# Loading the first third of an image-rotation kernel as four runs of consecutive rows, and storing it as four transfers

## The chip, the cores and the metric

The kernel runs on one core of one Trainium2 chip. The metric is the device time of one execution in microseconds (us). Before the change three executions took 122.31, 122.42 and 122.51 us, so the median is 122.42 us.

## The reference

The input is 32 images of 3 channels, each plane 256 x 256 in fp32: 96 planes of 65,536 values, 25.17 MB. The reference turns every plane by 180 degrees:

```python
def reference(x):
    return np.rot90(x, k=2, axes=(-2, -1)).astype(np.float32)
```

A turn by 180 degrees of a plane in row-major order is nothing but the plane's 65,536 values in reverse order. Every byte is read once from HBM and written once, so 50.33 MB must move.

## The kernel before

The 96 planes are cut into three groups of 32 (`G = 32`). A plane is cut into four quarters of `E = 16384` values, 64 KiB each, and a quarter is called a row here. A group is then 128 rows, one for each partition of SBUF: row 4n + s is quarter s of plane n. Three tiles A, B (`Bt`) and C (`Ct`) of 128 partitions x 16384 values hold the three groups, and a small tile T of 128 x 2048 is scratch. All four lie in SBUF at the same time, so no group waits for a buffer.

Two steps make the turn. Inside a row, VectorE reverses the 16384 values in place. `swap(t, lo, w)` does it for one pair of column blocks, in three copies (line 52): the upper block backwards into T, the lower block backwards into the upper one's place, and T into the lower one's place. `inside(t)` does four such swaps, each of `J = 2048` columns. Between rows, the store reverses the order of the four quarters of a plane: its HBM side is `o4[g][:, ::-1, lo:hi]`, three nested indices, 32 planes by 4 quarters (backwards) by the columns.

The first group is loaded by four transfers (line 73), each with every fourth row, into every fourth partition; two are issued by SyncE's queue (SP in the profile) and two by ScalarE's (ACT). Partition p receives row p. The loads of B and C (line 55) are one transfer of 128 rows each, on SP's queue.

VectorE's copies are kept in program order. It does three whole swaps of A and part of the fourth, then all of B, then the last 1152 columns on each side of A (`LAST = 1152`), then all of C. The stores (line 58) are all issued by SP, in program order: a strip of A of 128 columns, 512 B of each row (`LEAD = 128`), which needs only the first swap of A; then the other 16256 columns of A, which need the last copy of A and so stand behind all of B's swaps; then B; then C. A store waits on SP for the copies and loads that it needs, and everything behind it on SP waits with it.

Of the kernel before, what the change touches and what calls it, by code (L numbers as in the profile page):

```python
# [2 lines left out]

os.environ.setdefault("NEURON_RT_ULTRASERVER_MODE", "4")

# [4 lines left out]


@with_exitstack
def kernel(
    ctx: ExitStack,
    tc: tile.TileContext,
    x: bass.AP,
    out: bass.AP,
):

    nc = tc.nc
    P = 128

    B, C, H, W = x.shape
    L = H * W
    G = 32
    E = L // 4
    J = E // 8

    x4 = x.rearrange("b c h w -> (b c) (h w)").rearrange(
        "(g n) (s e) -> g (n s) e", n=G, s=4)
    o4 = out.rearrange("b c h w -> (b c) (h w)").rearrange(
        "(g n) (s e) -> g n s e", n=G, s=4)  # L40

    pool = ctx.enter_context(tc.tile_pool(name="slots", bufs=1))
    A = pool.tile([P, E], x.dtype, tag="A")
    Bt = pool.tile([P, E], x.dtype, tag="B")
    Ct = pool.tile([P, E], x.dtype, tag="C")
    T = pool.tile([P, J], x.dtype, tag="T")

    def back(t, lo, hi):
        return t[:, hi - 1:(lo - 1 if lo else None):-1]

    def copy(dst, src):
        tc.keep_in_program_order(nc.vector.tensor_copy(out=dst, in_=src))  # L52

    def load(t, g, lo, hi, queue=nc.sync):
        return queue.dma_start(out=t[:, lo:hi], in_=x4[g][:, lo:hi])

    def store(t, g, lo, hi):
        return nc.sync.dma_start(
            out=o4[g][:, ::-1, lo:hi], in_=t[:, lo:hi])

    def swap(t, lo, w):
        hi = E - lo - w
        copy(T[:, 0:w], back(t, hi, hi + w))
        copy(t[:, hi:hi + w], back(t, lo, lo + w))
        copy(t[:, lo:lo + w], T[:, 0:w])

    def inside(t):
        for lo in range(0, E // 2, J):
            swap(t, lo, J)

    SPLIT = 4
    for i in range(SPLIT):
        (nc.sync, nc.scalar)[i % 2].dma_start(  # L73
            out=A[i::SPLIT, :], in_=x4[0][i::SPLIT, :])
    load(Bt, 1, 0, E)
    load(Ct, 2, 0, E)
    LAST = 1152
    LEAD = 128
    for lo in range(0, E // 2 - J, J):
        swap(A, lo, J)  # L80
    swap(A, E // 2 - J, J - LAST)
    store(A, 0, 0, LEAD)
    inside(Bt)
    swap(A, E // 2 - LAST, LAST)
    store(A, 0, LEAD, E)
    store(Bt, 1, 0, E)
    inside(Ct)
    store(Ct, 2, 0, E)


# [1 line left out]
_INS = ['x']  # L92
_OUTS = [((32, 3, 256, 256), 'float32')]


# [23 lines left out]
```

## Time and profile before

| what | value |
|---|---|
| median of three executions | 122.42 us |
| the profiled execution's own time | 122.3 us |
| span of its trace | 120.5 us |
| VectorE busy | 44.6 us (37%) |
| bytes moved | 50.33 MB |
| mean rate over the span | 418 GB/s |

Only two kinds of work show in the page: VectorE's 39 copies and the transfers. The span is the time between the first and the last record of the program; 1.8 us of the profiled execution's time lie around it. The page's row of DMA digits gives the mean busy share of the core's 16 DMA engines in 40 slices. The row of rates below it is in lumps, because a 64 KiB packet counts where it starts, so a rate is to be read over many microseconds. A packet is one contiguous piece that a DMA engine moves; the smallest ones, under 512 B, are the marks by which the engines report that their share of a transfer is done.

### The profile page before, as it was taken

The page shows a single profiled execution, that of the slowest core. Times are in us where ns is not written, and L with a number is a line of the kernel's source. Part 1 is how long each engine was busy: PE and PEld are TensorE (multiplying, and loading weights), DVE is VectorE, ACT ScalarE, POOL GpSimd, SP SyncE. Part 2 cuts the span into 40 slices and gives each one's busy share as a digit, 9 for nine tenths or more (in the row PEclk, how much of TensorE's full clock was granted, in tenths as well). Part 3 has the DMA queues.
Part 4 walks back from the last instruction along what each step waited for, and adds up shares of the span by engine and source line. Part 5 has one row for each costly group of instructions (what it writes and reads, how often), then busy time and mean ns, then how long its engine had stood idle before and what let it go on. Part 6 is the DMA issues. An engine that isn't in the chain of part 4 may idle for free.

```text
span 120.5 us, 101 instructions
## 1 busy us (share of the span) xinstructions
DVE 44.6 (37%) x39; POOL 0.2 (0%) x4
## 2 busy tenths in 40 slices
DVE  0000000299991099999849999500000000000000
POOL 0000000000000000000000000000000000000000
DMA  9888998899889988998889777988898889888980
GB/s 348 348 348 348 522 522 348 348 479 566 348 348 479 566 348 348 479 566 348 348 367 691 345 345 345 691 348 348 348 696 348 348 348 696 348 348 348 674 370 0
DMA packets 1056, 50.33 MB, mean 418 GB/s; under 512 B 160, under 2 KB 288, under 8 KB 288
## 3 DMA queue, kind: packets, MB, share of 16 engines
q1 hardware_dynamic: 960, 46.14, 88.5%
q10 hardware_dynamic: 96, 4.19, 8.6%
HBM read 25.17 MB, written 25.17 MB: 418 GB/s over the span
## 4 chain that ended last, share of the span: by engine, by line
DMA 33%; DVE 27%; another core or an unknown queue 1%; SPq 1%; issue 1%; DVEq 0%
DMA Bt<-in_x_dram 33%; DVE T L52 9%; DVE Bt L52 8%; DVE Ct L52 8%; DVE A L52 1%; SPq L73 1%; DVEq L52 0%
## 5 line engine op out<-in xcount | busy, mean ns | idle before, releaser
L52 DVE COPY T<-A 128x2048 f32<-128x2048 f32 (+2 forms) x5 | 5.1, 1014 | 23.4 <-DMA A<-in_x_dram 23.3
L52 DVE COPY T<-Bt 128x2048 f32<-128x2048 f32 x4 | 4.9, 1227 | 5.9 <-DMA Bt<-in_x_dram 5.8
L52 DVE COPY T<-Ct 128x2048 f32<-128x2048 f32 x4 | 4.9, 1227 | 2.0 <-DMA Ct<-in_x_dram 1.9
L52 DVE COPY A<-T 128x2048 f32<-128x2048 f32 (+2 forms) x5 | 5.1, 1013 | 0.2
L52 DVE COPY A<-A 128x2048 f32<-128x2048 f32 (+2 forms) x5 | 5.1, 1013 | 0.2
L52 DVE COPY Bt<-Bt 128x2048 f32<-128x2048 f32 x4 | 4.9, 1227 | 0.1
L52 DVE COPY Bt<-T 128x2048 f32<-128x2048 f32 x4 | 4.9, 1227 | 0.1
L52 DVE COPY Ct<-T 128x2048 f32<-128x2048 f32 x4 | 4.9, 1227 | 0.1
L52 DVE COPY Ct<-Ct 128x2048 f32<-128x2048 f32 x4 | 4.9, 1226 | 0.1
L103 POOL MEMSET const-bfloat16-1.0<- 128x1 bf16 x1 | 0.1, 101 | 0.0
L103 POOL MEMSET const-uint8-127<- 128x1 uint8 x1 | 0.1, 101 | 0.0
L103 POOL MEMSET const-float32-0.0<- 128x1 f32 x1 | 0.1, 98 | 0.2 <-issue 0.2
L103 POOL MEMSET const-float32-1.0<- 128x1 f32 x1 | 0.1, 98 | 0.0
## 6 DMA issues: line engine op xcount, KB each, us to landing
out_dram<-A SPq DMA_DIRECT2D x1, 8128.0 KB, 21.1
out_dram<-A SPq DMA_DIRECT2D x1, 64.0 KB, 34.8
A<-in_x_dram ACTq DMA_DIRECT2D x2, 17.1
A<-in_x_dram SPq DMA_DIRECT2D x2, 17.3
Bt<-in_x_dram SPq DMA_DIRECT2D x1, 40.1
Ct<-in_x_dram SPq DMA_DIRECT2D x1, 58.8
out_dram<-Bt SPq DMA_DIRECT2D x1, 39.8
out_dram<-Ct SPq DMA_DIRECT2D x1, 42.7
```

Source lines behind the costliest of these rows:

```text
L52: tc.keep_in_program_order(nc.vector.tensor_copy(out=dst, in_=src))
L73: (nc.sync, nc.scalar)[i % 2].dma_start(out=A[i::SPLIT, :], in_=x4[0][i::SPLIT, :])
L103: nc = _bacc.Bacc("TRN2", target_bir_lowering=False, num_devices=1)
```

## The change

The four loads of A still fill every fourth partition each, but load i now reads 32 consecutive rows of the input, rows 32i to 32i + 31, that is planes 8i to 8i + 7. So partition 4k + i now holds row 32i + k, where before partition p held row p.

Because the planes now lie elsewhere in A, one transfer can no longer store A as before. Four transfers store it, all issued by SP after A's last swap: transfer i takes the 32 partitions i, i + 4, i + 8, ... and writes planes 8i to 8i + 7, again with the four quarters of each plane backwards. Its HBM side is 8 planes by 4 quarters by 16384 values. The 512 B strip is gone, and whole rows are stored. VectorE's copies, the loads and stores of B and C and the queues are as before.

```diff
     SPLIT = 4
     for i in range(SPLIT):
         (nc.sync, nc.scalar)[i % 2].dma_start(
-            out=A[i::SPLIT, :], in_=x4[0][i::SPLIT, :])
+            out=A[i::SPLIT, :], in_=x4[0][i * G:(i + 1) * G, :])
     load(Bt, 1, 0, E)
     load(Ct, 2, 0, E)
     LAST = 1152
-    LEAD = 128
     for lo in range(0, E // 2 - J, J):
         swap(A, lo, J)
     swap(A, E // 2 - J, J - LAST)
-    store(A, 0, 0, LEAD)
     inside(Bt)
     swap(A, E // 2 - LAST, LAST)
-    store(A, 0, LEAD, E)
+    N = G // SPLIT
+    for i in range(SPLIT):
+        nc.sync.dma_start(
+            out=o4[0][i * N:(i + 1) * N, ::-1, :], in_=A[i::SPLIT, :])
     store(Bt, 1, 0, E)
     inside(Ct)
     store(Ct, 2, 0, E)
```

## The prediction

> **What bounds the kernel now.** I read the page first: shares of the engines, the 40 slices, the packet counts, and the list of DMA issues.
>
> ```profile
> span 120.5 us, 101 instructions
> DVE 44.6 (37%) x39; POOL 0.2 (0%) x4
> ...
> DMA  9888998899889988998889777988898889888980
> ...
> DMA packets 1056, 50.33 MB, mean 418 GB/s; under 512 B 160, under 2 KB 288, under 8 KB 288
> ```
>
> VectorE works 37% of the span; the DMA digits stay at 7 to 9 from the first slice to the last but one. So the transfers bound the kernel throughout. The last line will matter most. This kernel issues ten transfers (four loads of A, one each of B and C, two stores of A, one each of B and C), and 160 packets are under 512 B: 16 for each transfer, one for each DMA engine. The 128 packets of exactly 512 B are the strip, the difference between 160 and 288. What remains, 768, are the rows: 6 passes of 128.
>
> The stretches of the trace give the pace (the last two columns are the mean busy share of the 16 engines and the rate):
>
> ```profile
> 4.00:19.00 15.00, 0.00 (x0) 0.00 (x0) 1.00 0.97 419
> ...
> 24.00:36.00 12.00, 11.62 (x12) 0.00 (x0) 1.00 1.01 437
> ...
> 60.50:61.20 0.70, 0.00 (x0) 0.00 (x0) 1.00 1.56 625
> ...
> 82.00:116.00 34.00, 0.00 (x0) 0.00 (x0) 1.00 1.00 432
> ```
>
> Loads (4 to 36 us) and stores (82 to 116 us) run at one pace, 432 GB/s at a share of 1.00: 27.0 GB/s for an engine, and 65,536 B by that is 2.43 us for one row on one engine. Around 61 us, where loads end and stores begin, no engine shows a hole (the share above 1 is the lumps of packets counted where they start).
>
> The issues and the order on SP's queue say when each third lands:
>
> ```profile
> out_dram<-A SPq DMA_DIRECT2D x1, 8128.0 KB, 21.1
> out_dram<-A SPq DMA_DIRECT2D x1, 64.0 KB, 34.8
> A<-in_x_dram ACTq DMA_DIRECT2D x2, 17.1
> ...
> Ct<-in_x_dram SPq DMA_DIRECT2D x1, 58.8
> out_dram<-Bt SPq DMA_DIRECT2D x1, 39.8
> out_dram<-Ct SPq DMA_DIRECT2D x1, 42.7
> ```
>
> ```profile
> 2.89 0.47 SPq L55 DMA_DIRECT2D Ct<-in_x_dram  x1
> ...
> 59.13 0.76 DVE L52 COPY A<-T 128x1152 f32<-128x1152 f32 x1
> 59.92 0.57 SPq L58 DMA_DIRECT2D out_dram<-A  x1
> 60.53 0.60 SPq L58 DMA_DIRECT2D out_dram<-Bt  x1
> ...
> 76.92 0.54 SPq L58 DMA_DIRECT2D out_dram<-Ct  x1
> ```
>
> C's load lands at 2.89 + 58.8 = 61.7, A's store at 59.92 + 21.1 = 81.0, B's at 60.53 + 39.8 = 100.3, C's at 76.92 + 42.7 = 119.6. Each stored third takes 19.3 us: 128 rows over 16 engines are 8 rows each, 8 x 2.42 = 19.3. The transfers of one queue go through in the order of issue, and each is issued well before its turn. Nothing but the engines' pace and how evenly rows are dealt over them sets the end.
>
> **The change part by part.** I sum against the profiled execution: span 120.5 us, 1.8 us around it, 122.3 us, which is 0.1 us under the median.
>
> *Loads of A from consecutive rows.* Same packets, same partitions, same queues; only the HBM addresses differ. The nearest rows are the loads of B and C, which read consecutive rows: 437 GB/s against 419 for A. The 8.39 MB of A take 20.0 us at 419 and 19.2 at 437, so a gain of up to 0.8 us; no row shows a loss, and I allow the same 0.8. I take 0, since at 419 the engines are already 0.97 busy.
>
> *The strip.* Its 64 KiB move with the whole rows instead, and 128 packets, 16 marks and one issue of SP go. At the pace above 64 KiB are 0.15 us. Against that, the strip lay ready in the queue behind C's load and covered the joint. A's store is issued at 59.92. The kernel's first load is issued at 0.73 and nothing moves before 2 us, about 1.3 us later, so stores may start about 61.2, and the loads land up to 61.7. Bounds -0.2 to +0.5 us; I take 0.
>
> *Issues on SP.* In the changed program's order on SP, where one store of A stood after the last swap there are now four. The first waits for VectorE's last copy of A, at the same 59.9 us, since no VectorE instruction is moved; the other three wait besides only for loads long landed. At 0.6 us each (0.57 and 0.60 above) they end at 62.3, so B's store is issued about 1.8 us later. B's rows are behind A's on any engine that has A's rows: one of the new transfers is at least 2 rows, 4.8 us, and covers three issues of 1.8 us. C's store waits for VectorE until 76.9, as before. Cost 0, unless some engines get no row of A; those would idle about 2 us, but they would also be far ahead.
>
> *How the new stores are dealt.* This is the term that counts. The outermost index of the transfers before is 32 or 128 on both sides: 32 x 4 planes and quarters against 128 partitions in the stores, 32 against 32 or 128 against 128 rows in the loads. All are multiples of 16, and all left 16 marks. In the changed program a store of A is 8 x 4 x 16384 on its HBM side and 32 rows on its SBUF side. No row of this trace shows an outermost 8. Lower bound: the 32 rows are dealt over 16 engines, as in the four loads of A, 2 each, and the cost is 0. Upper bound with rows at their present pace: planes are dealt whole, 8 engines take 4 rows each and the other 8 none. Four such transfers give the eight 16 rows instead of 8: 8 more x 2.42 = +19.3 us. The rest of the kernel does not return this, because B's and C's rows are dealt evenly and the eight busy engines still have 8 rows of each to do: from 61.3 they have 16 + 8 + 8 = 32 rows, 77.4 us, to about 138.7, against 24 before. The other eight finish near 63.6 + 16 x 2.42 = 102 and stand idle. I take the upper value: the nearest row in form is the store of B, whose outermost index on the HBM side is the plane, and there 32 planes are two whole planes for each engine; nothing in the trace shows a plane cut between engines.
>
> [...]
>
> *Sum.* 122.3 + 0 + 0 + 0 + 19.3 = 141.6 us.
>
> **The rivals.**
>
> *Rows are still dealt over 16 engines.* For it: the loads of A, the same 32 rows and partitions, did so. Against it: their outermost index is 32 on both sides. The point that decides is the number of marks of a new store, 16 or 8. Then only the small terms remain: 122.3 us, between 121.3 and 123.6. This is the case that is not slower.
>
> *Eight engines, and they get in each other's way in SBUF.* With planes dealt whole, engine c reads partitions 16c + i, then 4, 8 and 12 further, all eight in step and at few places at a time. If two share a path that carries one engine's 27.0 GB/s, a row of A takes 4.84 us while they collide: 16 x 2.42 = +38.7 us more at most for pairs, 180.3 us. Against it: the loads of A also touch every fourth partition and lose nothing (419 GB/s at 0.97). For it: those were spread over 16 engines by a deal that the trace does not show. Anything between 142 and 180 is possible, as far as engines fall out of step.
>
> [...]
>
> *Eight engines, but 432 GB/s is a limit of all together.* Then the eight would go faster once the others are idle, from about 102 us. They have 15 rows left each; in half the time that gives back 18 us: 123.5 us. Against it: an engine is busy 1.00 of the time at its 27.0, with no waiting that another's idleness could remove.
>
> **How the numbers follow.** Chances: the forecast 0.52, collisions 0.33, 16 engines 0.10, the shared limit 0.05. The forecast alone has 140.8 to 143 us: its small terms are -0.8 - 0.2 and +0.8 + 0.5. The range must take in most of the collisions: 140 to 181 us leaves out the 0.15 of the two fast cases and some 0.05 of collisions by more than pairs. A difference under 0.2% is what a measurement here can't tell from none. Slower takes the forecast, collisions and the shared limit, 0.90; the case of 16 engines is split into faster 0.04, same 0.04 and slower 0.02: together faster 0.04, same 0.04, slower 0.92.
>
> **What would show it.** In the profile after, packets under 512 B: twelve transfers would leave 192 with 16 engines each, 160 if the four stores of A leave 8 each. The DMA digits stay at 9 until about 102 us and then fall to 5, at about 216 GB/s, until the end. The stores of A land about 99 us, B's at 119, C's at 138.7. If instead A's stores land at 138 the collisions are there; if they land at 81 the deal is over 16. VectorE's copies must stand where they stood. The prediction is wrong if the marks are 192, or if the rows' pace after 61 us is not 27.0 GB/s for each busy engine.

## The result

The changed kernel takes 179.44 us (median of four executions, 179.35 to 179.66) against 122.45 us in the same comparison. The ratio is 1.4659, with a 95% interval of 1.4634 to 1.4685. The time lies inside the range of 140 to 181 us, near its upper end, but the loss is 57.0 us where 19.3 were forecast.

The page of the changed kernel:

```profile
span 177.9 us, 102 instructions
DVE 44.6 (25%) x39; POOL 0.2 (0%) x4
...
DMA  7999799999799909998999889954544543222120
...
DMA packets 928, 50.33 MB, mean 283 GB/s; under 512 B 160, under 2 KB 160, under 8 KB 160
```

VectorE's work is the same 44.6 us. The marks are 160, not 192: eight transfers with 16 marks and four with 8, so each new store runs on eight engines. The DMA digits fall to 5 after some 115 us and then to 2 from some 150 us: first eight engines, then four still have rows to do.

The stretches of its trace (the last two columns are the mean busy share of the 16 engines and the rate in GB/s):

```profile
4.00:19.00 15.00, 0.00 (x0) 0.00 (x0) 1.00 0.97 419
...
61.50:66.50 5.00, 4.13 (x4) 0.00 (x0) 1.00 0.51 105
...
72.00:100.00 28.00, 5.23 (x5) 0.00 (x0) 1.00 0.98 309
...
120.00:140.00 20.00, 0.00 (x0) 0.00 (x0) 1.00 0.50 213
150.00:172.00 22.00, 0.00 (x0) 0.00 (x0) 1.00 0.25 110
```

Two of these lines have the same share and not the same rate. From 61.5 to 66.5 us, when A's stores have begun and B's have not, eight engines are busy and move 105 GB/s, 13 GB/s each. From 120 to 140 us eight engines are busy and move 213 GB/s, 27 each. So busy engines do not move at one pace: right after 61.5 us each row takes twice as long. From 72 to 100 us all sixteen are busy, eight with A and eight with B and C, at 309 GB/s where such a stretch had 432 before.

The issues:

```profile
Ct<-in_x_dram SPq DMA_DIRECT2D x1, 59.1
out_dram<-Bt SPq DMA_DIRECT2D x1, 90.5
out_dram<-Ct SPq DMA_DIRECT2D x1, 99.5
```

```profile
60.44 6.58 SPq L85 DMA_DIRECT2D out_dram<-A  x4
...
67.06 2.63 SPq L58 DMA_DIRECT2D out_dram<-Bt  x1
...
77.40 0.57 SPq L58 DMA_DIRECT2D out_dram<-Ct  x1
```

B's store lands at 67.06 + 90.5 = 157.6 us and C's at 77.40 + 99.5 = 176.9: 19.3 us apart, as before. Going back another 19.3 us, the last engine was done with A at about 138.3, where 100.0 would be the end at the full pace (61.3 + 16 x 2.42). The loads end where they did, within 0.6 us. So all of the loss lies in A's stores: they last 77 us on the slowest engine, a mean of 4.8 us for a row.

The mean hides the course. The trace also keeps the time of every packet, and each row's packet begins where another one ends, so the rows of one engine can be followed. On the engine that ends last the first two rows take 5.1 and 5.3 us, the next six 7.0 to 8.4 us, and all 24 after them 2.42 us each. Altogether 21 rows take over 6 us. They lie on the four engines that end last, and all of them begin between 71 and 112 us, while the rows of B and C run on the other eight engines (from 70.4 to some 120 us).

### The profile page after: what moved, and what is told of

Same layout as the page of the kernel before. It is cut to its first block, busy times and chain, and to the rows that moved or that the text cites. A ratio compares the mean times of both kernels' runs of the same rounds, so it can differ in the third digit from the quotient of the medians.

```text
span 177.9 us, 102 instructions
## 1 busy us (share of the span) xinstructions
DVE 44.6 (25%) x39; POOL 0.2 (0%) x4
## 5 line engine op out<-in xcount | busy, mean ns | idle before, releaser
L52 DVE COPY T<-A 128x2048 f32<-128x2048 f32 (+2 forms) x5 | 5.1, 1013 | 23.9 <-DMA A<-in_x_dram 23.8
## 6 DMA issues: line engine op xcount, KB each, us to landing
out_dram<-Bt SPq DMA_DIRECT2D x1, 90.5
out_dram<-Ct SPq DMA_DIRECT2D x1, 99.5
```

## The experiments

One theory and three rivals stood at this point. Theory: the eight engines of one new store, and those that store B beside them, read SBUF at partitions that share a path. Rivals: the HBM side (eight engines writing planes 256 KiB apart), the loads' new order, or four small transfers as such.

**The loads alone.**

```diff
-            out=A[i::SPLIT, :], in_=x4[0][i::SPLIT, :])
+            out=A[i::SPLIT, :], in_=x4[0][i * G:(i + 1) * G, :])
```

with the strip and the store of A as before.

> The loads of A read consecutive rows as in the changed kernel; A is stored as before, strip and then one transfer with 32 planes outermost (so A's planes go out in another order than the reference wants). If the new addresses of the loads matter by no more than the 0.5 us by which VectorE's first copy starts later after the change (23.8 against 23.3 us), this takes 122.4 to 123.0 us. If the loads' order is what costs, it takes 130 us or more.

Measured 122.53 us, ratio 1.0013 (1.0003 to 1.0022). The loads' order costs 0.16 us by the ratio.

**Four stores, 32 rows outermost.** To the changed kernel:

```diff
+    r4 = out.rearrange("b c h w -> (b c) (h w)").rearrange(
+        "(g n) (s e) -> g (n s) e", n=G, s=4)
...
-            out=o4[0][i * N:(i + 1) * N, ::-1, :], in_=A[i::SPLIT, :])
+            out=r4[0][i * G:(i + 1) * G, :], in_=A[i::SPLIT, :])
```

> The changed kernel with the same four stores of A, the same partitions and the same 2 MB of HBM each, but the HBM side written as 32 rows in place of 8 planes by 4 quarters (the quarters of A are not turned round, which is left out). If the outermost 8 narrows a store to eight engines and everything follows from that, this takes 122.3 to 123.2 us, with 192 packets under 512 B. If the cost lies in having four transfers of 32 partitions, in every fourth partition, or in SP's issues, it stays between 140 and 180 us.

Measured 122.73 us, ratio 1.0027 (1.0011 to 1.0043), with these packets:

```profile
DMA packets 960, 50.33 MB, mean 416 GB/s; under 512 B 192, under 2 KB 192, under 8 KB 192
```

The same four pieces of 2 MB, from the same partitions, cost next to nothing once the outermost size is 32: 192 marks, sixteen engines each. The whole loss hangs on the outermost 8.

**Eight engines, neighbouring partitions.** To the changed kernel:

```diff
-            out=A[i::SPLIT, :], in_=x4[0][i * G:(i + 1) * G, :])
+            out=A[i::SPLIT, :], in_=x4[0][i::SPLIT, :])
...
-            out=o4[0][i * N:(i + 1) * N, ::-1, :], in_=A[i::SPLIT, :])
+            out=o4[0][i * N:(i + 1) * N, ::-1, :], in_=A[i * G:(i + 1) * G, :])
```

> The loads of before (partition p holds row p); four stores of 8 planes each, as in the changed kernel on the HBM side, but from 32 neighbouring partitions, so that each engine reads four neighbouring partitions and no two of the eight read 32 apart. Theory, paired places in SBUF: the eight no longer slow each other, the narrow deal remains, and only the last two stores of A (partitions 64 to 127) can meet the stores of B on the other eight engines; 141.6 us if they do not meet, about 161 us if they share by halves while they meet. The rate just after 62 us is 216 GB/s at a share of 0.5. Rival, the HBM side (eight engines writing planes 256 KiB apart): HBM is addressed exactly as after the change, so the rate after 62 us is 105 GB/s at 0.5 and the time stays near 179 us.

Measured 163.19 us, ratio 1.3339 (1.3317 to 1.3361). HBM is written exactly as in the changed kernel, on eight engines too, and 16 us of the loss are gone. The time is near the 161 us that were expected if A's last two stores and B's rows share by halves while they meet. The rival of the HBM side falls. The stretches of this run show what is left:

```profile
62.00:78.00 16.00, 14.44 (x12) 0.00 (x0) 1.00 0.84 360
82.00:118.00 36.00, 0.00 (x0) 0.00 (x0) 1.00 0.99 204
```

Until 78 us A's first two stores (partitions 0 to 63) run beside B's store at a rate that fits the share (0.84 of 432 is 363). From 82 to 118 us, with A's other two stores (partitions 64 to 127), all sixteen engines are busy at less than half the rate: there each row takes 4.7 to 5.4 us.

**Five ways to store A, with nothing beside them.** Each way starts when the one before it has landed, through a one-column copy into A (`after_all()`; the calls between the ways are left out here):

```python
    for i in range(4):        # 1
        nc.sync.dma_start(out=o4[0][i * 8:(i + 1) * 8, ::-1, :], in_=A[i::4, :])
    for i in range(4):        # 2
        nc.sync.dma_start(out=o4[1][i * 8:(i + 1) * 8, ::-1, :], in_=A[i * G:(i + 1) * G, :])
    for i in range(4):        # 3
        nc.sync.dma_start(out=r4[2][i * G:(i + 1) * G, :], in_=A[i::4, :])
    for i in range(2):        # 4
        nc.sync.dma_start(out=o4[0][i * 16:(i + 1) * 16, ::-1, :], in_=A[i::2, :])
    store(A, 1, 0, E)         # 5
```

> Five ways to store the 8.39 MB of A, one after another with nothing beside them, each separated by a wait for the one before (nothing is reversed, the content is not the reference's). 1: as in the changed kernel, 8 planes from every fourth partition. 2: 8 planes from 32 neighbouring partitions. 3: 32 rows from every fourth partition. 4: two transfers of 16 planes from every second partition. 5: one transfer as before the change. Theory, paired places: 77 us for 1 if the pairs stay in step (eight engines at half pace) and less if they fall out of step, 38.7 us for 2, 19.3 us for 3 and 5, and up to 38.7 us for 4, where sixteen engines read, two at a time 32 partitions apart. Rival, HBM side: 1 and 2 alike, 4 and 5 alike. Rival, narrow deal alone: 38.7, 38.7, 19.3, 19.3, 19.3 us, and the loss of the changed kernel would come only from B's stores beside A's.

The timeline of this run, where each copy ends one way, and the brackets hold VectorE's wait for it:

```profile
73.93 0.15 DVE L52 COPY A<-T 128x1 f32<-128x1 f32 x1 [51.08 <-DMA out_dram<-A]
...
115.00 0.15 DVE L52 COPY A<-T 128x1 f32<-128x1 f32 x1 [40.92 <-DMA out_dram<-A]
...
136.50 0.15 DVE L52 COPY A<-T 128x1 f32<-128x1 f32 x1 [21.35 <-DMA out_dram<-A]
...
177.37 0.15 DVE L52 COPY A<-T 128x1 f32<-128x1 f32 x1 [40.72 <-DMA out_dram<-A]
177.56 0.57 SPq L58 DMA_DIRECT2D out_dram<-A  x1
```

Way 3 waits 21.35 us: 19.3 for the rows, some 2 for issue and landing. Way 5, the single store of before, is issued at 177.56, and the span ends at 199.5, 21.9 us later: the full pace too. Way 2, eight engines from neighbouring partitions, takes 19.6 us more: the narrow deal, at the forecast's price. Way 1, the changed kernel's, takes another 10.2 us. Way 4 is the telling one: sixteen planes outermost, and still 40.72, with rows of up to 5.4 us. If each engine takes a whole plane, the sixteen read in pairs 32 partitions apart, and the doubled time would come from these pairs even though no engine is without rows. That is the author's reading, since the trace names no partition. But way 1 should have taken 77 us if its pairs had stayed in step; it waits 51.08.

**Two engines alone.** Three stores of 2 planes in each of five phases, from 8 partitions that lie 1, 2, 4, 8 and 16 apart (`after_all()` as above):

```python
    for step in (1, 2, 4, 8, 16):
        after_all()
        for k in range(3):
            nc.sync.dma_start(
                out=o4[n // 32][n % 32:n % 32 + 2, ::-1, :],
                in_=A[0:7 * step + 1:step, :])
            n += 2
```

> Two engines alone: A is loaded, and then five phases, each waiting for the one before, of three stores of 2 planes from 8 partitions, which lie 1, 2, 4, 8 and 16 apart (nothing is reversed and most of the output is not written). Each engine reads 12 rows of a phase, the two always 4, 8, 16, 32 and 64 partitions apart, on the same HBM addresses' pattern in all phases. If places are paired 32 apart and nowhere else, four phases take 12 x 2.42 = 29 us and some 2.3 us of issue and landing, and the fourth (32 apart) up to 58 us, less if the two fall out of step. If any two engines that read few partitions slow each other, all five are slow.

```profile
53.67 0.15 DVE L52 COPY A<-T 128x1 f32<-128x1 f32 x1 [30.88 <-DMA out_dram<-A]
84.97 0.15 DVE L52 COPY A<-T 128x1 f32<-128x1 f32 x1 [31.14 <-DMA out_dram<-A]
116.44 0.15 DVE L52 COPY A<-T 128x1 f32<-128x1 f32 x1 [31.32 <-DMA out_dram<-A]
157.02 0.15 DVE L52 COPY A<-T 128x1 f32<-128x1 f32 x1 [40.43 <-DMA out_dram<-A]
```

The distances are those of the author's reading, a whole plane of four rows for each engine: 4, 8, 16, 32 and 64 partitions. Two engines 4, 8 and 16 apart take 31 us, and 32 apart 40.4. The stretches below show the first phase, three parts of the fourth, and the fifth, in which 64 apart again moves 56 GB/s. Of these distances only 32 costs time, with 26 GB/s for the pair at first. Inside the fourth phase the two drift out of step:

```profile
24.00:52.00 28.00, 0.00 (x0) 0.00 (x0) 1.00 0.13 56
118.00:128.00 10.00, 0.00 (x0) 0.00 (x0) 1.00 0.10 26
128.00:140.00 12.00, 0.00 (x0) 0.00 (x0) 1.00 0.11 38
140.00:154.00 14.00, 0.00 (x0) 0.00 (x0) 1.00 0.11 47
158.00:186.00 28.00, 0.00 (x0) 0.00 (x0) 1.00 0.13 56
```

The pair together moves 26 GB/s at first, one engine's worth, then 38, then 47. The packets show the same: the first row of each takes over 5 us, the last ones 2.42, and one engine ends at 154.1 us, the other at 156.6, one row later. By then one engine has got ahead by a row.

**A's stores by themselves in the kernel.** To the changed kernel:

```diff
-    store(Bt, 1, 0, E)
     inside(Ct)
+    copy(A[:, 0:1], T[:, 0:1])
+    copy(T[:, 0:1], Bt[:, 0:1])
+    copy(Bt[:, 0:1], T[:, 0:1])
+    copy(T[:, 0:1], Ct[:, 0:1])
+    copy(Ct[:, 0:1], T[:, 0:1])
+    store(Bt, 1, 0, E)
     store(Ct, 2, 0, E)
```

> The changed kernel with the stores of B and C held back until all four stores of A have landed (five one-column copies on VectorE between them, which rewrite one column of A, so that the store of it is waited for, and of B and C with their own values). Theory: in the phases run the same four stores of A took 51.2 us by themselves, from their first issue to the next phase's, so most of what A's stores lose in the changed kernel comes from B's stores on the other eight engines, which read the same places. Then, from the issue at 60.4 us: 51.2 + 0.5 + 41.2 (two stores over sixteen engines, 38.7, and 2.5 for issue and landing) is a span of 153.3 and a time of 155 us: holding transfers back makes the kernel 24 us faster. Rival, the eight engines' pairs alone cost it all: A's stores still land near 138 us and the time is about 182 us.

Measured 155.53 us, ratio 1.2703 (1.2683 to 1.2722), span 153.4. The kernel with less overlap is 23.9 us faster than the changed one. A's last store has landed when VectorE's first held copy starts:

```profile
60.23 6.58 SPq L85 DMA_DIRECT2D out_dram<-A  x4
...
111.28 0.15 DVE L52 COPY A<-T 128x1 f32<-128x1 f32 x1 [34.12 <-DMA out_dram<-A]
...
111.84 0.61 SPq L58 DMA_DIRECT2D out_dram<-Bt  x1
```

That is 51.1 us after the first issue, against 77.9 us (60.44 to about 138.3) when B's and C's rows are read beside them. No row takes over 5.3 us here, where 8.4 was the longest in the changed kernel.

**The same with neighbouring partitions.** The five copies in the kernel that takes 163.2 us.

> The same holding back, with the four stores of A from 32 neighbouring partitions (163.2 us without it). Theory: the narrow deal alone is left; 59.9 + 41.1 (phase 2 of the phases run) + 0.5 + 41.2 is a span of 142.7 and a time of 144.5 us. Rival, the rows of 5.1 us after 80.8 us in that run come from the partitions 64 to 127 themselves and not from meeting B's: about 166 us.

Measured 145.23 us, ratio 1.1866 (1.1849 to 1.1882), span 143.1. With B held back, the engines keep 206 GB/s at a share of 0.48 from 62 to 98 us, 26.8 for each busy engine. The slow stretch after 82 us was B's and A's rows meeting, not the partitions 64 to 127 themselves.

**The strip.**

```diff
-    LEAD = 128
...
-    store(A, 0, 0, LEAD)
...
-    store(A, 0, LEAD, E)
+    store(A, 0, 0, E)
```

> The kernel before without the strip: A stored whole in one transfer after its last swap. The forecast's term for the strip was 0, between -0.2 and +0.5 us: 122.2 to 122.9 us.

Measured 122.50 us, ratio 1.0010 (1.0001 to 1.0019): 0.1 us.

**Four stores by quarters.** To the changed kernel:

```diff
-            out=A[i::SPLIT, :], in_=x4[0][i * G:(i + 1) * G, :])
+            out=A[i::SPLIT, :], in_=x4[0][i::SPLIT, :])
...
-    N = G // SPLIT
...
-            out=o4[0][i * N:(i + 1) * N, ::-1, :], in_=A[i::SPLIT, :])
+            out=o4[0][:, SPLIT - 1 - i, :], in_=A[i::SPLIT, :])
```

> The loads of before (transfer i of A holds quarter i of all 32 planes in partitions i, i + 4, ...) and four stores of A, each of one quarter of all 32 planes, so that 32 is outermost and the quarters are turned round by the address alone. If the outermost size is all that matters, four stores cost nothing: 122.3 to 122.8 us, with 192 packets under 512 B. If four stores of every fourth partition cost by themselves, 125 us or more.

Measured 122.67 us, ratio 1.0020 (1.0011 to 1.0029). Here the four stores turn the quarters round by the address alone, and 32 planes remain outermost: A can be stored in four pieces without the loss, if it is cut by quarter and not by plane. No kernel tried is faster than the one before.

## Why the prediction was right in part and wrong in size

*What bounds the kernel* held: the transfers do, and VectorE's time did not move.

*The loads* were taken at 0, and cost 0.16 us. *The strip* was taken at 0; leaving it out costs 0.1 us. *The issues on SP* were taken at 0.6 us each. They took 6.58 us for four in the changed kernel, and B's store was issued 6.5 us later than before, where 1.8 was forecast. That did not set the end, because the eight engines without rows of A were done with B and C by some 120 us. With 32 rows outermost, where the four issues took 3.93 us, the kernel stays within 0.4 us of the one before.

*How the new stores are dealt*, first half: right. The marks are 160, eight engines take four rows of each store, sixteen in all, and the narrow deal by itself costs 19.6 us in the phases run where 19.3 were worked out. At an outermost 2 the marks narrow likewise: the run with two engines has 46 packets under 512 B, 16 for its load and 2 for each of its 15 stores, and a busy share of 0.13.

The step that failed is the price of a row in that same term: "8 more x 2.42 = +19.3 us" keeps the old pace for all sixteen rows of A. The prediction's own sign of being wrong came: after 61.5 us each busy engine moves 13 GB/s and not 27.0. The slowest engine needed a mean of 4.8 us: two rows at 5.1 and 5.3 us, six at 7.0 to 8.4, and eight at the old 2.42. The forecast had collisions as its second rival, eight engines in each other's way in SBUF, at 0.33, and priced them at 180.3 us at most; 179.4 was measured. But that agreement of size is chance. The rival's price was pairs in step, 4.84 us for every row to the end. Hardly a row of the slowest engine took that: slower and faster ones happen to average to it. Held back and side by side, the runs show another split:

- the narrow deal: 19.3 us;
- every fourth partition in place of neighbouring ones, read here as pairs 32 apart among the eight: 155.53 - 145.23 = 10.3 us, not the 38.7 of pairs that stay in step;
- the rows of B and C read beside them: the remaining 57.0 - 19.3 - 10.3 = 27.4 us, or directly, 77.9 - 51.1 = 26.8 us of A's stores.

Why the forecast ranked it second: it used the loads of A, which touch the same every fourth partition at 419 GB/s, as evidence against collisions. Way 3 of the phases run shows the mistake. The same partitions run at the full pace, 21.35 us with issue and landing, when 32 rows are outermost, and way 1 takes 51.08. So the partitions alone do not set the pace. The author's reading is that it matters which engines are at which partition at the same moment, and that this changed with the outermost size; no trace names an engine's partition. With planes dealt whole, the rival already had engine c at partition 16c + i. Which of these places slow each other no row of before shows, and the rival left it at "few places at a time"; the distance of 32 was measured only afterwards, with two engines.

The forecast left some 0.05 for collisions by more than pairs. That a third reader joined the pairs is shown in part. Rows of 7.0 to 8.4 us are longer than any in the runs where, by the same reading, only two should meet: 5.4 us at most in way 4 and in the kernel with neighbouring partitions, 5.3 us for two engines alone. They occur only while the rows of B and C run, and never when those are held back. What stays open is which rows met there and how the place was divided among them: the trace names neither the engine nor the partition of a packet, and no run has three engines at one place by themselves.

The rival of sixteen engines fell with the 160 marks. That of a common limit fell too: in the last stretch four engines move 110 GB/s, 27.5 each, no faster for the others' idleness.

## What to carry to other kernels

Before cutting a transfer into pieces, look at the outermost size of each side and count the marks. Here pieces of 32 rows with 8 planes outermost left 8 marks and kept eight engines busy (share 0.51), with 32 outermost 16 marks, and the cut along the quarters cost 0.2 us. Then write down which partitions the engines may read at the same moment. Here two engines, 32 partitions apart by the author's reading, moved 26 GB/s together at first, against 56 at 4 and 64 apart. The busy share hid it, 0.10 against 0.13 there and 0.51 at 105 GB/s in the changed kernel, so read the rate beside the share. Where a group of transfers uses only some engines, ask what the transfers beside it cost: holding them back gained 24 us here.

## What the runs showed that was not expected

The two slow engines did not stay in step. In the two-engine run the pair's rate rises from 26 to 47 GB/s within some 30 us, so the loss of this pair is 9 us and not 29. With sixteen planes outermost (way 4) no such recovery shows in the time, 40.7 us against some 41 for staying in step (twice 19.3, and some 2 for issue and landing). In the kernel with neighbouring partitions, too, the eight rows of A that each engine reads after some 80 us stay at 4.8 to 5.4 us to the last. Why these pairs stay together and the others part was not tried.

Issuing also got slower: SP needed 6.58 us for four stores of A in the changed kernel, and 2.63 for B's, against 0.6 each before. Slow rows are only a part of it. In the kernel with neighbouring partitions the same four took 4.44 us, and with 32 rows outermost 3.93, though there every row ran at the full pace. What the issue waits for stays open.
